# Taking the sum of a left operand one product ahead, in the down products of a two-layer decoder trunk

## The chip, the cores and the metric

The kernel runs on one core of one Trainium2 chip. The metric is the device time of one execution in microseconds (us), the median over the runs. Beside the timed runs there is one profiled execution; all rows of the trace come from it.

## The reference, cut to what matters

The program is a decoder trunk with two layers, 512 positions, a model width of 1024 and a feed-forward width of 2816, all in float32. Each layer is a mixer (a gated convolution with sliding-window attention in layer 0, gated linear attention with latent attention in layer 1), a layer norm, a SwiGLU feed-forward block and a second layer norm. What the change touches is the last matrix product of the feed-forward block:

```
def swiglu(x, w_gate, w_up, w_down):
    return (jax.nn.silu(x @ w_gate) * (x @ w_up)) @ w_down
...
x = layer_norm(ALPHA * x + swiglu(x, ffn_w_gate[layer], ffn_w_up[layer], ffn_w_down[layer]), ...)
```

Every product is made nearly exact by splitting both operands: hi is the operand rounded to TensorE's fp32r type, lo is what the rounding left, and hi x hi + hi x lo + lo x hi is accumulated.

## The kernel before, in words

**The feed-forward block.** The hidden width of 2816 is 22 tiles of 128. Tiles 0 and 1 are computed directly, the other 20 as 10 pairs by a scheme in which seven products of half-size blocks stand for eight (`sevens`, lines 650 to 770; its matmuls are on L713). The results, the hidden tiles, lie in `hs`, each 128 x 512, some in the pool `wk` and some in a large tile that the trace calls `m`.

**The down products.** `seven_down` (L532) multiplies hidden pairs 0 to 7 by their rows of `w_down` by the same kind of scheme. They form four quads q = 0 to 3. For each quad, `hs[DIRECT + q]` gives the blocks a11 and a21 and `hs[DIRECT + QUADS + q]` gives a12 and a22. There are seven products for each quad, named by a position pos, 28 in all, in the order of `seq` (L542). I number them i = 0 to 27:

```
        seq = [(2, 0), (2, 1), (1, 0), (1, 1), (2, 2), (5, 0), (1, 2), (5, 1), (1, 3), (2, 3), (5, 2), (6, 0),
               (5, 3), (6, 1), (6, 2), (6, 3), (3, 0), (3, 1), (3, 2), (3, 3), (7, 0), (7, 1), (7, 2), (7, 3),
               (4, 0), (4, 1), (4, 2), (4, 3)]
```

The left operand of positions 1, 2 and 4 is a block as it is (a11, a12, a22). That of positions 5, 6, 3 and 7 is a sum of blocks, and in 16 of the 28 products VectorE therefore has a sum to take first. For positions 5, 6 and 3 it is kept in place in one of four slices of a tile `ssum` (position 5 sets a22 - a21, position 6 adds a11, position 3 subtracts a12); for position 7 it is a fresh tile from the pool `tmp`. Between i = 10 and i = 23 every product has a sum. `ssum` takes over the buffer of `xl0`, the lo part of the block's input, when `sevens` has done with it.

**make(i), L571.** It prepares both operands of product i. On SyncE's queue, `load(i + 4)` starts the transfer of a piece of weights into one of five `raw` buffers. Then the instructions are, in this order:

- ScalarE: hi of the weights, 128 x 1024 (L100, `w<-raw`)
- VectorE: lo of the weights, 128 x 1024 (L106, `w<-raw,w`)
- VectorE: the sum, 128 x 512, where there is one (L585, L587, L589 or L592)
- ScalarE: hh, the hi part of the left operand, 128 x 512 (L100, or L594 for position 6, `hx<-...`)
- VectorE: hl, its lo part, 128 x 512 (L106, or L595)

**take(i), L600.** It is TensorE's part: 12 matmuls on L613 with 512 columns each, six into one PSUM bank (b = 0) and then six into another (b = 1). After the last quad of a position come copies out of these banks: for position 1 two to `tmp` (L628), for position 5 two to `p5` (L619), for positions 6 and 7 two from the bank into a fresh bank (L623), all on ScalarE; for positions 3 and 7 two on VectorE (L632), and for position 2 two more (L635). The copy of position 6 reads the two banks `d` into which position 3, the very next product, goes on to accumulate.

**The order.** In `ffn` (L450) the order of every engine and queue is the order in which the code is written. The loop at its end calls make(i) and then take(i - AHEAD), AHEAD = 4, so that on ScalarE the copies of take(i) stand behind all of make(i + 4). The operand pair hi and lo lies in a pool `wp` of five buffers, so make(i) can't start before take(i - 5) has ended; hh and hl lie in the pool `hx` of twelve. What comes behind (`down`, L336, with its matmuls on L349, and the mixer of the next layer) is ordered by hand on TensorE only; on the other engines a planner of the language arranges it by estimated costs and due times.

Of the kernel before, what the change touches and what calls it, by code (L numbers as in the profile page):

```python
# [11 lines left out]
F32R = mybir.dt.float32r  # L12
# [34 lines left out]
def trunk(ctx, tc, a, out):  # L47
# [22 lines left out]
    def nm(s):  # L70
        cnt[0] += 1
        return f"{s}{cnt[0]}"
# [4 lines left out]
    def slot2(dt=F32):  # L77
        return hx.tile([P, 512], dt, tag="hx", name=nm("hx"))

    def temp(tag="tmp", dt=F32):  # L80
        return tmp.tile([P, 512], dt, tag=tag, name=nm(tag))
# [4 lines left out]
    def ps():  # L86
        return psp.tile([P, 512], F32, tag="ps", name=nm("ps"))
# [11 lines left out]
    def split(src, hi, lo, pool=False):  # L99
        nc.scalar.copy(out=hi, in_=src)  # L100
        if pool:
            n = src.shape[1] // 2
            for c in (slice(0, n), slice(n, 2 * n)):
                nc.gpsimd.tensor_tensor(out=lo[:, c], in0=src[:, c], in1=hi[:, c].bitcast(F32), op=ALU.subtract)
            return
        tt(out=lo, in0=src, in1=hi.bitcast(F32), op=ALU.subtract)  # L106

    def pair(n=D):
        t = wp.tile([P, 2, D], F32R, tag="w", name=nm("w"))
        return t[:, 0, :n], t[:, 1, :n]  # L110
# [17 lines left out]
    def renew():  # L128
        for t, n in ((xh, "xh"), (xl, "xl")):
            t[:] = t or [None, None]  # L130
            for j in range(2):
                if t[j] is None:
                    t[j] = big.tile([P, 4, S], F32R, tag=f"{n}{j}", name=nm(n))
# [398 lines left out]
    def seven_down(hs):  # L532

        base = state["i"]
        state["i"] += 4 * QUADS
        raw, ops = {}, {}
        s_ = {}

        g = {}
# [4 lines that stand above are left out]
        def piece(which, q):  # L546
            i = base + 4 * q + ("11", "12", "21", "22").index(which)
            return a["w"][i // 2, :, (i % 2) * D:(i % 2) * D + D]


        t_ = {(n, q): dram.tile([P, D], F32, tag=f"t{n}{q}", name=nm("t")) for n in (1, 2, 3, 4) for q in range(QUADS)}

        def copy(n, q, src):
            nc.gpsimd.dma_start(out=t_[n, q], in_=piece(src, q) if isinstance(src, str) else t_[src, q])

        def add(n, q, which):
            nc.gpsimd.dma_start(out=t_[n, q], in_=piece(which, q), accum_op=ALU.add)

        steps = [lambda f=f, n=n, q=q, w=w: f(n, q, w)
                 for f, n, w in ((copy, 1, "11"), (add, 1, "12"), (copy, 3, "22"), (add, 3, "12"), (copy, 2, 1),  # L560
                                 (add, 2, "22"), (copy, 4, 2), (add, 4, "21")) for q in range(QUADS)]

        def load(i):
            if not 0 <= i < len(seq):
                return
            pos, q = seq[i]
            raw[i] = rawp.tile([P, D], F32, tag="raw", name=nm("raw"))
            src = {1: "11", 2: "21", 3: "22", 5: 1, 6: 2, 7: 3, 4: 4}[pos]
            nc.sync.dma_start(out=raw[i], in_=piece(src, q) if isinstance(src, str) else t_[src, q])

        def make(i):  # L571

            load(i + 4)
            if not s_:
                s = big.tile([P, 4, S], F32, tag="xl0", name=nm("ssum"))
                s_.update({q: s[:, q, :] for q in range(QUADS)})
                xl[0] = None
            pos, q = seq[i]
            (a11, a21), (a12, a22) = hs[DIRECT + q], hs[DIRECT + QUADS + q]
            hi, lo = pair()  # L580
            split(raw.pop(i), hi, lo)
            hh, hl = slot2(F32R), slot2(F32R)
            x = {1: a11, 2: a12, 4: a22, 7: None}.get(pos, s_.get(q))
            if pos == 5:
                tt(out=x, in0=a22, in1=a21, op=ALU.subtract)  # L585
            elif pos == 6:
                tt(out=x, in0=x, in1=a11, op=ALU.add)  # L587
            elif pos == 3:
                tt(out=x, in0=x, in1=a12, op=ALU.subtract)  # L589
            elif pos == 7:  # L590
                x = temp()
                tt(out=x, in0=a11, in1=a21, op=ALU.subtract)  # L592
            if pos == 6:
                act(out=hh, in_=x, func=AF.Copy, scale=-1.0)  # L594
                stt(out=hl, in0=x, scalar=-1.0, in1=hh.bitcast(F32), op0=ALU.mult, op1=ALU.subtract)  # L595
            else:
                split(x, hh, hl)
            ops[i] = hi, lo, hh, hl

        def take(i):  # L600

            pos, q = seq[i]
            hi, lo, hh, hl = ops.pop(i)
            name = {2: "a", 1: "d", 5: "b", 6: "d", 3: "d", 7: "e", 4: "f"}[pos]
            if name not in g:
                g[name] = [ps(), ps()]
            fresh = q == 0 and pos in (1, 2, 5)
            for b in range(2):
                bank = g[name][b]
                for k in range(2):  # L610
                    t, c = slice(k * 256 + b * P, k * 256 + b * P + P), slice(k * 512, k * 512 + 512)
                    for m, (l, r) in enumerate(((hh, hi), (hh, lo), (hl, hi))):
                        mm(bank, lhsT=l[:, t], rhs=r[:, c], start=(fresh and k == 0 and m == 0),  # L613
                           stop=(k == 1 and m == 2), skip_group_check=True)
                if q < QUADS - 1:
                    continue
                if pos == 5:
                    g.setdefault("p5", []).append(temp("p"))
                    nc.scalar.copy(out=g["p5"][b], in_=bank)  # L619
                elif pos in (6, 7):  # L620
                    to = "e" if pos == 6 else "f"
                    g.setdefault(to, []).append(ps())
                    nc.scalar.copy(out=g[to][b], in_=bank)  # L623
            if q == QUADS - 1:
                for b in range(2):
                    if pos == 1:
                        g["p1"] = temp()
                        nc.scalar.copy(out=g["p1"], in_=g["d"][b])  # L628
                        g.setdefault("sum", []).append((b, g["p1"]))
                    elif pos in (3, 7):  # L630
                        bank = g[name][b]
                        stt(out=bank, in0=bank, scalar=-1.0, in1=g["p5"][b], op0=ALU.mult, op1=ALU.subtract)  # L632
            if pos == 2 and q == QUADS - 1:
                for b, t in g["sum"]:
                    tt(out=g["a"][b], in0=g["a"][b], in1=t, op=ALU.add)  # L635

        acc = {}

        def last(f):
            f()  # L640
            renew()
            acc.update({b: [g["a"][b], g["d"][b]] for b in range(2)})
            acc.update({b + 2: [g["f"][b], g["e"][b]] for b in range(2)})

        n = len(seq)
        takes = [lambda i=i: take(i) for i in range(n)]
        takes[-1] = lambda: last(lambda: take(n - 1))
        return acc, [lambda i=i: make(i) for i in range(n)], takes, load, steps

    def sevens(sx, hs, hidden_tile):  # L650
# [787 lines left out]
```

## Time and profile before

| | |
|---|---|
| median of three runs | 1081.66 us (1081.38 to 1081.66) |
| profiled execution, device time | 1080.37 us |
| its span, first to last instruction | 1078.6 us |
| mean granted TensorE clock | 0.987 |
| TensorE matmul / weight load busy | 97% / 88% of the span |
| VectorE / ScalarE / GpSimd busy | 73% / 50% / 10% |
| matmuls of the down products (L613) | 672, in two stretches: 400.6 to 490.2 us and 948.5 to 1037.3 us |
| GpSimd in these two stretches | no instruction |

In the rows, PE is TensorE's matmul, PEld its weight load, DVE is VectorE, ACT ScalarE, POOL GpSimd, SPq SyncE's queue of transfers. A group of instructions reads "out<-in" by the program's names. In a timeline the columns are start, time covered, engine, line, operation, operands, count, and in brackets how long the engine sat idle before it and what released it. Instructions of an engine overlap a little, so the step from one start to the next is less than the duration. One product starts on TensorE every 2.73 us while nothing holds it.

### The profile page before, as it was taken

Reading aid. Unit: us, or ns where it says so; the run is one execution under the profiler, and the core shown is the slowest. Engines: PE = TensorE matmul, PEld = TensorE weight load, DVE = VectorE, ACT = ScalarE, POOL = GpSimd, SP = SyncE. Lnnn points to the kernel's source line nnn. Section 1 sums busy time; section 2 is a strip of 40 time slices with the busy share of each in tenths; the row PEclk is TensorE's granted clock in tenths of the full one; section 3 lists DMA queues with packets and bytes.
Section 4 is the critical chain, followed back from the end, with each engine's and each line's share of the span. In section 5 each row is a group of like instructions: output and inputs, shape, how many; then the busy total and the mean of one; then the engine's idle time right before and its main releaser. Section 6 shows DMA issues by size and latency. Waiting matters only on the chain.

```text
span 1078.6 us, 17142 instructions
## 1 busy us (share of the span) xinstructions
PE 1046.4 (97%) x6861; PEld 946.5 (88%) x6861; DVE 792.5 (73%) x1180; ACT 543.4 (50%) x896; POOL 103.5 (10%) x162
## 2 busy tenths in 40 slices
PE   9999999999999999599999999999999999997796
PEld 7888889999999998488988888889999999986685
DVE  5666549888787777684857886479887787786757
ACT  5544335655545465463467454355655554554541
POOL 0000001222000000000513420003120000000000
PEclk9999999999999999799999999999999999999899
DMA  9522222999624355453232031228997323364422
GB/s 335 203 77 79 78 79 61 286 300 286 180 80 136 99 165 187 138 172 101 98 137 78 2 118 36 76 68 221 310 310 216 115 79 124 113 234 136 140 76 78
DMA packets 42960, 156.60 MB, mean 145 GB/s; under 512 B 4976, under 2 KB 5632, under 8 KB 42624
## 3 DMA queue, kind: packets, MB, share of 16 engines
q1 hardware_dynamic: 35168, 120.89, 33.1%
q0 software_dynamic: 7712, 34.61, 12.7%
q8 instruction: 54, 0.88, 0.3%
q14 instruction: 26, 0.21, 0.1%
HBM read 153.38 MB, written 35.65 MB: 175 GB/s over the span
## 4 chain that ended last, share of the span: by engine, by line
PE 90%; DVE 5%; ACT 3%; issue 1%; DMA 0%; SPq 0%; POOL 0%; DVEq 0%; ACTq 0%; POOLq 0%
PE ps L713 37%; PE ps L193 16%; PE ps L349 13%; PE ps L613 9%; PE ps L227 6%; DVE w L106 2%; ACT w L100 2%; PE ps L1162 1%; PE ps L289 1%; PE ps L1087 1%; PE ps L1010 1%; PE ps L859 1%; PE ps L806 1%; PE ps L846 1%; PE ps L1060 0%
## 5 line engine op out<-in xcount | busy, mean ns | idle before, releaser
L106 DVE TENSOR_TENSOR w<-raw,w 128x1024 fp32r<-128x1024 f32 (+2 forms) x206 | 249.2, 1214 | 77.3 <-ACT w L100 72.2
L100 ACT CAST w<-raw 128x1024 fp32r<-128x1024 f32 (+3 forms) x209 | 215.0, 1035 | 79.2 <-PE ps L713 17.0
L713 PE MATMUL ps<-xh,w 128*128 128x256 f32 x1280 | 237.5, 283 | 0.0
L713 PEld LDWEIGHTS ps<-xh,w 128*128 128x128 f32 x1280 | 202.7, 192 | 0.0
L713 PE MATMUL ps<-xl,w 128*128 128x256 f32 x640 | 181.1, 283 | 0.0
L713 PE MATMUL ps<-hx,w 128*128 128x256 f32 x1440 | 179.6, 283 | 0.0
L613 PE MATMUL ps<-w,hx 128*128 128x512 f32 x672 | 156.8, 396 | 21.9 <-ACT ps L623 21.9
L713 PEld LDWEIGHTS ps<-hx,w 128*128 128x128 f32 x1440 | 175.9, 192 | 0.1
L613 PEld LDWEIGHTS ps<-w,hx 128*128 128x128 f32 x672 | 128.4, 192 | 49.7 <-ACT ps L623 22.8
L193 PE MATMUL ps<-xh,w 128*128 128x512 f32 (+1 forms) x608 | 161.0, 348 | 0.2 <-ACT xh L100 0.2
L349 PE MATMUL ps<-w,hx 128*128 128x512 f32 x657 | 151.9, 391 | 0.0
L349 PEld LDWEIGHTS ps<-w,hx 128*128 128x128 f32 x657 | 122.7, 188 | 25.1
L713 PEld LDWEIGHTS ps<-xl,w 128*128 128x128 f32 x640 | 122.8, 192 | 0.3
L193 PEld LDWEIGHTS ps<-xh,w 128*128 128x128 f32 x608 | 106.4, 189 | 15.3 <-ACT xh L100 0.7
L193 PE MATMUL ps<-xl,w 128*128 128x512 f32 (+1 forms) x304 | 105.0, 345 | 0.2 <-DVE xl L106 0.2
L266 POOL TENSOR_TENSOR rs<-ve,neghalf 128x1 f32<-128x1 f32 x15 | 9.2, 611 | 713.5 <-DVE ve L264 675.2
L193 PEld LDWEIGHTS ps<-xl,w 128*128 128x128 f32 x304 | 57.6, 190 | 7.2 <-DVE xl L106 0.8
L227 PE MATMUL ps<-w,xh 128*128 128x512 f32 (+1 forms) x192 | 58.6, 386 | 0.0
L106 DVE TENSOR_TENSOR w<-lnb,w 128x1024 fp32r<-128x1024 f32 x30 | 36.7, 1225 | 17.8 <-ACT w L100 17.7
L106 DVE TENSOR_TENSOR w<-lng,w 128x1024 fp32r<-128x1024 f32 x30 | 36.7, 1224 | 16.4 <-ACT w L100 16.4
L106 DVE TENSOR_TENSOR hx<-m,hx 128x512 fp32r<-128x512 f32 x32 | 21.3, 688 | 31.8 <-ACT hx L100 31.8
L227 PEld LDWEIGHTS ps<-w,xh 128*128 128x128 f32 x192 | 35.2, 188 | 5.0
(249 smaller groups left out, 1244.2 us busy)
## 6 DMA issues: line engine op xcount, KB each, us to landing
raw<-in_w_dram SPq DMA_DIRECT2D x174, 512.0 KB, 4.8
t<-in_w_dram POOLq DMA_DIRECT2D x48, 512.0 KB, 11.1
raw<-t SPq DMA_DIRECT2D x32, 512.0 KB, 3.3
t<-t POOLq DMA_DIRECT2D x16, 512.0 KB, 13.0
hx<-in_xT_dram SPq DMA_DIRECT2D x8, 256.0 KB, 6.2
xn<-in_xn_dram SPq DMA_DIRECT2D x4, 512.0 KB, 9.4
out_dram<-xn SPq DMA_DIRECT2D x7, 256.0 KB, 2.0
lng<-in_ln_mix_g_dram SPq DMA_DIRECT2D x2, 512.0 KB, 7.5
```

Of the source, the lines that this page charges most:

```text
L100: nc.scalar.copy(out=hi, in_=src)
L106: tt(out=lo, in0=src, in1=hi.bitcast(F32), op=ALU.subtract)
L193: mm(dst[:, cols], lhsT=l[:, k, :], rhs=xk(r, k, cols), start=(k == 0 and n == 0), stop=(k == KD - 1 and n == 2))
L227: mm(banks[b][:, :n], lhsT=xk(l, k, t), rhs=r[:, c], start=(k == 0 and m == 0), stop=(k == KD - 1 and m == 2))
L289: nc.tensor.transpose(tp[:, k * P:(k + 1) * P], xn[:, b, h * 512 + k * P:h * 512 + (k + 1) * P], ident)
L349: mm(acc[b][h], lhsT=l(b), rhs=r[:, h * 512:h * 512 + 512], start=(not begun and k == 0 and n == 0), stop=(k == ends[b, h] and n == 2), sk ...
L613: mm(bank, lhsT=l[:, t], rhs=r[:, c], start=(fresh and k == 0 and m == 0), stop=(k == 1 and m == 2), skip_group_check=True)
L713: mm(bank[:, f * 256:f * 256 + 256], lhsT=l[:, f, k, :], rhs=r[k // 2][:, k % 2, :], start=(start and f == 0 and k == 0 and m == 0), stop= ...
L806: mm(banks[s][bank][:, o:o + n], lhsT=l[rows[s], b * P:(b + 1) * P], rhs=r[rows[s], (b + 1) * P - n:(b + 1) * P], start=(i == 0), stop=(i ...
L846: nc.tensor.transpose(bank[:, o:o + P], src, ident)
L859: mm(po[rows[s], b * P:(b + 1) * P], lhsT=vn[:, j * P + 64 * s:j * P + 64 * s + 64], rhs=loc[s][(b, half)], start=(half == 0 or b == 0), s ...
L1010: mm(dst, lhsT=x[:, c], rhs=y, start=(k == 0 and n == 0), stop=(k == nk - 1 and n == 2))
```

## The change

`make` is cut in two. The sum of product i is taken by a new function `total(i)`, and make(i) calls total(i + 1) between its own lo of the weights and its own hh. The result waits in a dictionary `left` until make(i + 1) uses it. make(0) calls total(0) itself, and the buffer `ssum` is now taken in the first `total`. VectorE's order in make(i) is then lo of the weights i, sum of product i + 1, hl of product i. In the order of the program, hh of product i stands behind the sum of product i + 1. No instruction is added or removed, and nothing else changes its place.

```diff
-        def make(i):
-
-            load(i + 4)
+        left = {}
+
+        def total(i):
+
+            if i >= len(seq):
+                return
             if not s_:
                 s = big.tile([P, 4, S], F32, tag="xl0", name=nm("ssum"))
                 s_.update({q: s[:, q, :] for q in range(QUADS)})
                 xl[0] = None
             pos, q = seq[i]
             (a11, a21), (a12, a22) = hs[DIRECT + q], hs[DIRECT + QUADS + q]
-            hi, lo = pair()
-            split(raw.pop(i), hi, lo)
-            hh, hl = slot2(F32R), slot2(F32R)
-            x = {1: a11, 2: a12, 4: a22, 7: None}.get(pos, s_.get(q))
+            x = {1: a11, 2: a12, 4: a22}.get(pos, s_[q])
             if pos == 5:
                 tt(out=x, in0=a22, in1=a21, op=ALU.subtract)
             elif pos == 6:
...
             elif pos == 7:
                 x = temp()
                 tt(out=x, in0=a11, in1=a21, op=ALU.subtract)
+            left[i] = x
+
+        def make(i):
+
+            load(i + 4)
+            pos, q = seq[i]
+            hi, lo = pair()
+            split(raw.pop(i), hi, lo)
+            if i == 0:
+                total(0)
+            x = left.pop(i)
+            total(i + 1)
+            hh, hl = slot2(F32R), slot2(F32R)
             if pos == 6:
                 act(out=hh, in_=x, func=AF.Copy, scale=-1.0)
                 stt(out=hl, in0=x, scalar=-1.0, in1=hh.bitcast(F32), op0=ALU.mult, op1=ALU.subtract)
```

## The prediction

> **What bounds the kernel now.** I read the page first, then the waits of the whole run, then the timeline of the two stretches in which the down products run, then the engine windows around them. The page says that TensorE sets the time:
>
> ```profile
> span 1078.6 us, 17142 instructions
> ...
> PE 1046.4 (97%) x6861; PEld 946.5 (88%) x6861; DVE 792.5 (73%) x1180; ACT 543.4 (50%) x896; POOL 103.5 (10%) x162
> ...
> PE 90%; DVE 5%; ACT 3%; issue 1%; DMA 0%; SPq 0%; POOL 0%; DVEq 0%; ACTq 0%; POOLq 0%
> ...
> L613 PE MATMUL ps<-w,hx 128*128 128x512 f32 x672 | 156.8, 396 | 21.9 <-ACT ps L623 21.9
> ```
>
> TensorE is busy for 97% of the span, yet the chain that ended last runs over DVE and ACT for 8% of it, and the down products' matmuls stand idle for 21.9 us behind a copy on ScalarE, L623. The waits tell how often, and what ScalarE itself waited for:
>
> ```profile
> PE ps L613 <- ACT ps L623: 21.9, 2, 11.0
> ...
> ACT hx L594 <- DVE ssum L587: 16.9, 8, 2.8
> ...
> ACT hx L100 <- DVE tmp L592: 15.2, 8, 1.9
> ACT hx L100 <- DVE ssum L585: 15.2, 8, 1.9
> ACT hx L100 <- DVE ssum L589: 15.2, 8, 1.9
> ```
>
> So there are two stalls of 11 us, one in each layer, and ScalarE waited 32 times for a sum on VectorE before an hh, once for each product with a sum. The timeline of layer 1 shows how the one makes the other:
>
> ```profile
> 948.51 43.71 PE L613 MATMUL ps<-w,hx 128*128 128x512 f32 x192
> ...
> 951.45 1.06 ACT L100 CAST w<-raw 128x1024 fp32r<-128x1024 f32 x1 [0.63 <-PE ps L613]
> ...
> 965.10 1.05 ACT L100 CAST w<-raw 128x1024 fp32r<-128x1024 f32 x1 [1.14 <-issue]
> ...
> 995.63 1.04 ACT L100 CAST w<-raw 128x1024 fp32r<-128x1024 f32 x1
> ...
> 999.09 1.04 ACT L100 CAST w<-raw 128x1024 fp32r<-128x1024 f32 x1
> ...
> 1000.16 1.23 DVE L106 TENSOR_TENSOR w<-raw,w 128x1024 fp32r<-128x1024 f32 x1 [0.25 <-ACT w L100]
> 1001.30 0.69 DVE L589 TENSOR_TENSOR ssum<-ssum,m 128x512 f32<-128x512 f32 x1
> 1002.02 0.62 ACT L100 CAST hx<-ssum 128x512 fp32r<-128x512 f32 x1 [1.90 <-DVE ssum L589]
> 1002.54 1.06 ACT L623 COPY ps<-ps 128x512 f32<-128x512 f32 x2
> 1002.67 0.69 DVE L106 TENSOR_TENSOR hx<-ssum,hx 128x512 fp32r<-128x512 f32 x1 [0.68 <-ACT hx L100]
> 1003.18 34.27 PE L613 MATMUL ps<-w,hx 128*128 128x512 f32 x144 [10.96 <-ACT ps L623]
> ```
>
> TensorE does 16 products in 43.71 us, 2.73 each. The hi casts at 951.45 (i = 5) and 965.10 (i = 10) start 0.2 us after take(0) and take(5) end (948.51 + 2.73 and + 6 x 2.73): so far make is as early as its five buffers allow. From i = 10 on every product has a sum, and then a ring holds: hi, lo of the weights, sum, hh, next hi. The last two casts of the row, i = 18 and 19, are 3.46 us apart. ScalarE thus loses 0.73 us per product against TensorE, and more at its copies. When TensorE ends take(15), at 948.51 + 43.71 = 992.2, ScalarE isn't even at make(18). The copies of take(15) stand behind make(19), take(16) writes into the bank they read, and TensorE waits until the first is done at 1003.18. The stall isn't a lack of prepared operands; it is the lateness of ScalarE's queue. It costs the clock as well:
>
> ```profile
> 455.23 35.11 PE L613 MATMUL ps<-w,hx 128*128 128x512 f32 x144 [10.97 <-ACT ps L623]
> ```
>
> ```profile
> 300.00:400.00 100.00, 100.00 (x836) 100.00 (x835) 76.67 (x76) 53.34 (x69) 0.00 (x0) 1.00 0.35 114
> 444.30:455.20 10.90, 0.00 (x0) 0.00 (x0) 7.34 (x9) 5.22 (x9) 0.00 (x0) 0.59 0.39 129
> 455.20:466.10 10.90, 10.87 (x38) 8.82 (x39) 6.33 (x8) 4.67 (x6) 0.00 (x0) 0.79 0.35 131
> ```
>
> The granted clock (the column before the last two) is 1.00 in a busy stretch, 0.59 in the stall and 0.79 in the 10.9 us behind it. The 144 matmuls after the stall should take 144/192 x 43.71 = 32.78 us; they took 35.11 and 34.27, which is 2.33 and 1.49 more.
>
> **The change part by part.** Nothing is added or removed: 32 sums of 0.69 us move on VectorE, each to the place after the lo of the weights of the product before. No transfer moves: load(i + 4) stays first in make(i), and neither SyncE's nor GpSimd's queue is passed.
>
> *ScalarE.* hh(i) now uses a sum taken one product earlier, so it can follow hi(i) at once. The steps of a make and of the copies without such a wait stand in the trace, at position 4:
>
> ```profile
> 1023.93 1.06 ACT L100 CAST w<-raw 128x1024 fp32r<-128x1024 f32 x1 [1.15 <-issue]
> 1024.89 0.61 ACT L100 CAST hx<-m 128x512 fp32r<-128x512 f32 x1
> 1025.41 0.58 ACT L623 COPY ps<-ps 128x512 f32<-128x512 f32 x1
> ...
> 1026.61 0.57 ACT L623 COPY ps<-ps 128x512 f32<-128x512 f32 x1
> ```
>
> hi to hh is 0.96 us and hh to the next 0.52, together 1.48 per product against TensorE's 2.73. These are also the copies of position 7, the same pattern as those that stall, and TensorE runs through them (its 144 matmuls stand in one row): with make at its limit such copies cost nothing.
>
> *VectorE.* Its steps where nothing is waited for:
>
> ```profile
> 1018.13 0.69 DVE L106 TENSOR_TENSOR hx<-tmp,hx 128x512 fp32r<-128x512 f32 x1 [0.69 <-ACT hx L100]
> 1018.74 1.29 DVE L632 SCALAR_TENSOR_TENSOR ps<-ps,p 128x512 f32<-128x512 f32 x2
> 1019.93 1.22 DVE L106 TENSOR_TENSOR w<-raw,w 128x1024 fp32r<-128x1024 f32 x1
> 1021.07 0.69 DVE L106 TENSOR_TENSOR hx<-wk,hx 128x512 fp32r<-128x512 f32 x1
> 1021.67 1.22 DVE L106 TENSOR_TENSOR w<-raw,w 128x1024 fp32r<-128x1024 f32 x1
> ```
>
> lo of the weights to the next 1.14, a 512-column instruction to the next 0.61, hl to lo 0.60: 1.14 + 0.61 + 0.60 = 2.35 per product with a sum, 0.38 below TensorE's 2.73. The 0.68 before hl goes too, since hh(i) ends (0.96 + 0.62 = 1.58 after hi) before hl(i) can start (1.08 + 1.14 + 0.61 = 2.83; 1.08 is 999.09 to 1000.16). One burden comes between, the two additions of L635 behind make(13):
>
> ```profile
> 980.69 1.29 DVE L635 TENSOR_TENSOR ps<-ps,tmp 128x512 f32<-128x512 f32 x2
> ```
>
> 1.29 us, paid back at 0.38 a product in four products, before make(19).
>
> *New waits.* The sum now stands ahead of hl(i), which is 0.61 later. Behind it queue lo(i + 1) and so on; who waits for hl(i) is take(i). At the limit hl(10) ends 2.83 + 0.69 = 3.5 after hi, at 968.6, and take(10) starts at 948.51 + 10 x 2.73 = 975.8: 7 us of cover. Without it each of the 32 sums would cost up to 0.61. The first sum needs the buffer of `ssum`, whose last matmuls, those of `sevens`, lie before 948.5, while the sum falls at make(4), after 951. A raw piece must land within the time from its issue:
>
> ```profile
> raw<-in_w_dram SPq DMA_DIRECT2D x174, 512.0 KB, 4.8
> ...
> raw<-t SPq DMA_DIRECT2D x32, 512.0 KB, 3.3
> ```
>
> load(i + 4) is issued when lo(i - 1) frees its buffer, 2.3 us after hi(i - 1), and used five products later, 13.7 after it: over 11 us for 4.8. These three cost nothing.
>
> *At the stall.* take(14) ends at 948.51 + 15 x 2.73 = 989.5. hi(19) starts at 989.7 (999.09 now), hh(19) at 990.6 (its sum, in make(18), is done at about 989.8), the first copy at 991.2, done 991.7. take(16) wants that bank at 992.2. The second copy starts when take(15) ends, is done at 993.0, and is wanted half a product after 992.2, at 993.6. Spare: 0.5 and 0.6 us. Both stalls go, and the slow clock with them. What is late next is nothing on this path: from 1023.93 on, make is at its buffer limit in the trace of before too (that cast starts when take(22) ends), so the work behind is met in the same relative state. There a planner arranges DVE and ACT and may choose anew; I put this at nothing, with one product's 2.73 us either way as bound.
>
> *Sum.* 10.97 + 10.96 of idle time and 2.33 + 1.49 of slow matmuls, 25.75 us. The profiled execution took 1080.37 us, 1.8 beyond its span; its span becomes 1052.9 and its time 1054.6. The median is 1.3 above that execution, so 1081.66 - 25.75 = 1055.9 us.
>
> **The rivals.** *VectorE becomes the bound.* The Trainium skill, "VectorE: DVE Perf Modes", section "The DRAIN you can't avoid", says that the next VectorE instruction does not start until the pipeline has emptied; the rows above do not bear it out to the full duration, as L632 starts 0.61 after an hl of 0.69. As a mechanism here: full durations, 1.23 + 0.69 + 0.69, and the 0.25 before lo make 2.86, 0.13 over TensorE. Over nine products that is 1.2, with L635 2.5 us of lateness. hh(19) can be 0.8 late and the first copy 0.5 more; 1.2 of stall would remain in each layer, 1058.3. If instead the 0.68 before hl stayed (1.14 + 0.61 + 0.68 + 0.60 = 3.03), lateness is 9 x 0.30 + 1.29 = 4.0, the stall 2.7 per layer, and with a quarter of the clock's toll 1062. Against it: everything in the steps quoted.
>
> *The change doesn't do what it says.* `ssum` is one tile of four slices, and in program order hh(i) now stands behind the sum of i + 1, which writes another slice. If waits went by the whole tile, hh(i) would wait for that sum, at the same place as now: the ring of 3.46 stays, ten products long as before, and the time is 1081.7. Against it stands layer 0's first products, where matmuls read token columns of `xh` while a cast ahead of them in program order writes others:
>
> ```profile
> 177.27 1.04 PE L289 MATMUL ps<-pack,xn 128*128 128x128 f32 x8
> ...
> 177.90 1.08 ACT L294 CAST xh<-ps 128x512 fp32r<-128x512 f32 x2 [2.75 <-PE ps L289]
> ...
> 178.06 0.36 PE L193 MATMUL ps<-xh,w 128*128 128x256 f32 x1
> ```
>
> L193 starts at 178.06, while the casts run until 178.98: waits go by region.
>
> *Slower: the clock.* The stalls are TensorE's rest. If the granted clock fell to the 0.79 of the row above in the longer unbroken run, each us would lose 0.21. At 80 us in each layer that is 34 us, 1089.5; it decides from 25.75 / 0.21 = 123 us in all. Against it: 1.00 over 100 us without a gap.
>
> **How the numbers follow.** Full effect 0.85, at 1055.9; VectorE bound 0.08, 1058 to 1062; no effect 0.05, 1081.7; slower 0.02. The range takes the planner's 2.73 below, 1053.2, and the VectorE rival's end above, 1062. About 0.2%, 2 us, is what a measurement of this kernel can tell from no change; faster by more 0.93, within it 0.05, slower 0.02.
>
> **What would show it.** Right: no idle time before L613, its 336 matmuls of a layer in one row of about 76.5 us, no ACT wait for L585, L587, L589 and L592, hh 0.96 after hi, a clock of 1.00 throughout these stretches. Wrong: a wait of hh for a sum at the old 1.9 (whole-tile rival), an idle time before L613 of 1 to 3 us with ACT waiting little (VectorE), or matmuls longer at a lower clock.

## The result, and the profile after

The median fell from 1081.66 us to 1054.70 us (four runs each; 1054.18 to 1055.51 after), a ratio of 0.9752 with a 95% interval of 0.9735 to 0.9769. The forecast was 1055.9, in a range of 1053.2 to 1062.0. The profiled execution took 1055.16 us, its span 1053.4. L613 of before is L626 now, L623 is L636, L635 is L648 and L594 is L607.

The lines of the page that answer to those of before:

```profile
span 1053.4 us, 17142 instructions
...
PE 1042.9 (99%) x6861; PEld 944.1 (90%) x6861; DVE 789.0 (75%) x1180; ACT 543.9 (52%) x896; POOL 103.3 (10%) x162
...
PE 97%; DVE 1%; DMA 1%; ACT 0%; SPq 0%; issue 0%; POOL 0%; DVEq 0%; ACTq 0%; POOLq 0%
...
L626 PE MATMUL ps<-w,hx 128*128 128x512 f32 x672 | 152.7, 389 | 0.0
```

The number of instructions is the same. The idle time before the down products' matmuls went from 21.9 us to none, their busy time from 156.8 to 152.7 us, and VectorE and ScalarE, which held 8% of the chain of waits, hold 1%. The timeline of layer 1 around the copies of product 15 shows how:

```profile
935.88 76.35 PE L626 MATMUL ps<-w,hx 128*128 128x512 f32 x336
...
964.50 1.29 DVE L648 TENSOR_TENSOR ps<-ps,tmp 128x512 f32<-128x512 f32 x2
965.70 1.22 DVE L106 TENSOR_TENSOR w<-raw,w 128x1024 fp32r<-128x1024 f32 x1
...
967.55 0.63 ACT L607 ACTIVATE hx<-ssum 128x512 fp32r<-128x512 f32 x1 [0.42 <-DVE ssum L587]
968.04 1.22 DVE L106 TENSOR_TENSOR w<-raw,w 128x1024 fp32r<-128x1024 f32 x1
...
970.38 1.22 DVE L106 TENSOR_TENSOR w<-raw,w 128x1024 fp32r<-128x1024 f32 x1
...
972.91 0.61 ACT L100 CAST hx<-ssum 128x512 fp32r<-128x512 f32 x1
...
974.19 0.68 DVE L589 TENSOR_TENSOR ssum<-ssum,m 128x512 f32<-128x512 f32 x1
...
976.95 1.05 ACT L100 CAST w<-raw 128x1024 fp32r<-128x1024 f32 x1 [1.15 <-issue]
...
977.91 0.61 ACT L100 CAST hx<-ssum 128x512 fp32r<-128x512 f32 x1
...
978.43 0.58 ACT L636 COPY ps<-ps 128x512 f32<-128x512 f32 x1
...
979.63 0.57 ACT L636 COPY ps<-ps 128x512 f32<-128x512 f32 x1 [0.62 <-PE ps L626]
```

All 336 matmuls of the layer stand in one row. ScalarE now idles 1.15 us before hi(19), at 976.95. The row names no releaser, but take(14), which frees the buffer that hi(19) needs, ends at 935.88 + 15 x 2.73 = 976.8: hi(19) is as early as it may be. The two copies are done at 979.0 and 980.2. At 76.35/28 = 2.73 us a product, TensorE wants the first bank at 935.88 + 16 x 2.73 = 979.5 and the second at 980.9. The second copy even waits for take(15) to end. Layer 0 has the same row, and the granted clock (before the last two columns) is full in both stretches:

```profile
401.02 76.35 PE L626 MATMUL ps<-w,hx 128*128 128x512 f32 x336
```

```profile
401.00:477.00 76.00, 76.00 (x338) 62.94 (x337) 65.77 (x82) 49.17 (x66) 0.00 (x0) 1.00 0.65 205
...
935.90:1012.00 76.10, 76.10 (x338) 63.02 (x337) 65.87 (x82) 49.18 (x66) 0.00 (x0) 1.00 0.61 193
```

From the first down product to the first matmul of what follows, layer 0 took 490.17 - 400.55 = 89.6 us and takes 477.21 - 401.02 = 76.2; layer 1 took 88.8 and takes 76.2. That is 13.4 + 12.6 = 26.0 us. The span fell by 25.2, since the rest of the kernel was 0.8 us slower in this execution, 0.5 of it before the first down product is reached.

### The profile page after: what moved, and what is told of

It reads as the page before. It is cut to its first block, busy times and chain, and to the rows that moved or that the text cites. A ratio compares the mean times of both kernels' runs of the same rounds, so it can differ in the third digit from the quotient of the medians.

```text
span 1053.4 us, 17142 instructions
## 1 busy us (share of the span) xinstructions
PE 1042.9 (99%) x6861; PEld 944.1 (90%) x6861; DVE 789.0 (75%) x1180; ACT 543.9 (52%) x896; POOL 103.3 (10%) x162
## 3 DMA queue, kind: packets, MB, share of 16 engines
q0 software_dynamic: 7712, 34.61, 13.1%
## 4 chain that ended last, share of the span: by engine, by line
PE 97%; DVE 1%; DMA 1%; ACT 0%; SPq 0%; issue 0%; POOL 0%; DVEq 0%; ACTq 0%; POOLq 0%
PE ps L726 38%; PE ps L193 16%; PE ps L626 14%; PE ps L349 13%; PE ps L227 6%; PE ps L1175 1%; PE ps L289 1%; PE ps L1100 1%; PE ps L1023 1%; PE ps L872 1%; DMA hx<-in_xT_dram 1%; PE ps L819 1%; PE ps L859 1%; PE ps L1073 0%; PE ps L1089 0%; PE ps L1071 0%
## 5 line engine op out<-in xcount | busy, mean ns | idle before, releaser
L626 PE MATMUL ps<-w,hx 128*128 128x512 f32 x672 | 152.7, 389 | 0.0
L349 PE MATMUL ps<-w,hx 128*128 128x512 f32 x657 | 151.9, 391 | 0.0
L626 PEld LDWEIGHTS ps<-w,hx 128*128 128x128 f32 x672 | 126.0, 188 | 26.1
L193 PEld LDWEIGHTS ps<-xh,w 128*128 128x128 f32 x608 | 106.3, 189 | 15.6 <-DVE w L106 0.4
```

Of the source, the lines that this page charges most:

```text
L193: mm(dst[:, cols], lhsT=l[:, k, :], rhs=xk(r, k, cols), start=(k == 0 and n == 0), stop=(k == KD - 1 and n == 2))
L349: mm(acc[b][h], lhsT=l(b), rhs=r[:, h * 512:h * 512 + 512], start=(not begun and k == 0 and n == 0), stop=(k == ends[b, h] and n == 2), sk ...
```

## The experiments

The theory that I tested I call the ring theory: ScalarE is made late by the ring hi, lo, sum, hh, hi in products 10 to 19, and TensorE feels it only where the copies of product 15 stand behind make(19). The first rival is that the gain comes by share, a part for each sum that an hh no longer waits for. Each run was compared with runs of the kernel before on the same chip, whose median was 1081.5 to 1081.8 us.

### Only the sums of position 7

```diff
-            if i == 0:
-                total(0)
+            if pos not in (7,):
+                total(i)
+            if i + 1 < len(seq) and seq[i + 1][0] in (7,):
+                total(i + 1)
             x = left.pop(i)
-            total(i + 1)
```

> Only the sums of position 7 (i = 20 to 23) are taken one product ahead; those of positions 5, 6 and 3 stand in their old place. Ring theory (what costs is how late ScalarE reaches the copies of product 15, which stand behind make(19)): these sums come after that point, so the idle time before the down products' matmuls stays at 11.0 us in each layer and the time at 1081.7, within 1.5. Rival, by share (each sum that an hh no longer waits for gives its part of the whole, 27.0/32 = 0.84 us): 8 sums, 6.7 us, 1074.9.

Measured: 1082.11 us, ratio 1.000 (0.9991 to 1.0009). The matmuls of the down products, as a group (busy time and mean ns, then idle time before them and its releaser), and the two stalls:

```profile
L627 PE MATMUL ps<-w,hx 128*128 128x512 f32 x672 | 157.6, 397 | 21.9 <-ACT ps L637 21.9
```

```profile
455.49 35.73 PE L627 MATMUL ps<-w,hx 128*128 128x512 f32 x144 [10.95 <-ACT ps L637]
...
1004.35 34.47 PE L627 MATMUL ps<-w,hx 128*128 128x512 f32 x144 [10.96 <-ACT ps L637]
```

The stalls are there in full. Eight hh no longer wait 1.9 us, and it is worth nothing: those products come after the copies that matter. The sharing rival falls.

### Only positions 5 and 6, only position 3

The same edit with (5, 6) and with (3,) in place of (7,).

> Only the sums of positions 5 and 6 (i = 5, 7, 10 to 15) are taken ahead; positions 3 and 7 keep the old order. Ring theory: make is at its buffer limit up to 16, then four rings with the copies of position 5 among them bring the first copy of product 15 to 14.8 us after hi(16), as before, where take(15) ends 10.7 after it; with 0.6 for the copy an idle time of about 4.7 us in each layer, 9.4 in all, and some of the slow clock behind it, 1 us a layer: 1066, within 1.5. Rival, by share: 16 of 32 sums, 13.5 us, 1068.2 with an idle time of 5.5 a layer. The two lie close here; the idle time and where it lies decide less than in the other runs.

> Only the sums of position 3 (i = 16 to 19) are taken ahead; 5, 6 and 7 keep the old order. Ring theory: the rings from 10 to 15 leave hi(16) 6.4 us behind its limit; from there ScalarE needs 2.5 and then VectorE 2.35 a product, so the copies come about 4.5 us after take(15) ends: idle 4.5 in each layer, 9 in all, and about 2 us of slow clock, 1065.7, within 2. Rival, by share: 8 sums, 6.7 us, 1074.9 with an idle time of about 8 a layer.

Measured: 1069.25 us (ratio 0.9886, 0.9872 to 0.9901) and 1068.61 us (0.9881, 0.9866 to 0.9895). First (5, 6), then (3,), each with its group and then the stalls in the timeline:

```profile
L627 PE MATMUL ps<-w,hx 128*128 128x512 f32 x672 | 159.0, 399 | 9.3 <-ACT ps L637 9.3
```

```profile
448.49 35.76 PE L627 MATMUL ps<-w,hx 128*128 128x512 f32 x144 [4.67 <-ACT ps L637]
...
991.09 35.80 PE L627 MATMUL ps<-w,hx 128*128 128x512 f32 x144 [4.67 <-ACT ps L637]
```

```profile
L627 PE MATMUL ps<-w,hx 128*128 128x512 f32 x672 | 157.1, 396 | 8.8 <-ACT ps L637 8.8
```

```profile
449.16 34.32 PE L627 MATMUL ps<-w,hx 128*128 128x512 f32 x144 [4.39 <-ACT ps L637]
...
989.72 35.31 PE L627 MATMUL ps<-w,hx 128*128 128x512 f32 x144 [4.37 <-ACT ps L637]
```

The idle times are those that the ring gives, 4.67 where 4.7 was expected and 4.4 where 4.5 was. For (3,) the sharing rival had about 8. Half of the sums and a quarter of them each take off more than half of the idle time, 12.6 and 13.1 us of 21.9, together more than the whole; no share can do that. But both times came out 3 us too long and outside what I had allowed (1.5 and 2 us), and for (5, 6) the time alone lies nearer to the rival's 1068.2; it is the idle time that speaks for the ring. The rows say where the 3 us are: the 144 matmuls behind the stall, 32.7 us at full clock (144/336 x 76.35), took 34.3 to 35.8. The slow clock cost 1.6 to 3.1 us a layer where I had put 1. A stall of 4.5 us costs the clock as much as one of 11.

### The copies earlier in ScalarE's queue, the sums as before

```diff
                 i -= AHEAD
                 if i < n:
                     take(i)
-                else:
+                elif i - n == 13:
+                    for j in (13, 14, 15):
+                        takes[j]()
+                elif i - n not in (14, 15):
                     takes[i - n]()
```

> The kernel before with its sums in the old place; only the takes of products 14 and 15 are written ahead of make(18), so that the two copies of product 15 stand behind make(17) in ScalarE's queue and not behind make(19). Ring theory: the copies start at 995.6 in layer 1 in place of 1002.5, the idle time at that point falls from 11.0 to about 4.0 us; but the ring goes on at 3.46 against 2.73, make(18) and (19) come 1 us later than before, and TensorE runs out of operands from about product 20: another 2 to 3 us of idle time spread before products 20 to 23, with hl or hh as releaser. In all 6.6 a layer in place of 11: 1071, within 3. Rival, the place in the queue is the whole cause: idle 4.0 a layer and nothing later, 1065 or less. Rival, the place doesn't matter, since preparation itself is what TensorE lacks: 1081.7.

Measured: 1081.06 us, ratio 0.9993 (0.9984 to 1.0003). The ring theory's 1071 missed by 10 us. The time is that of the last rival, 1081.7, but the rows show that its mechanism isn't what happened. The group, and TensorE's rows of layer 1:

```profile
L616 PE MATMUL ps<-w,hx 128*128 128x512 f32 x672 | 162.3, 404 | 15.9 <-ACT ps L626 15.8 <-ACT hx L100 0.2
```

```profile
949.57 43.71 PE L616 MATMUL ps<-w,hx 128*128 128x512 f32 x192
997.32 21.12 PE L616 MATMUL ps<-w,hx 128*128 128x512 f32 x84 [4.04 <-ACT ps L626]
1018.61 3.26 PE L616 MATMUL ps<-w,hx 128*128 128x512 f32 x12 [0.17 <-ACT hx L100]
1025.91 12.75 PE L616 MATMUL ps<-w,hx 128*128 128x512 f32 x48 [4.04 <-ACT ps L626]
```

The first stall fell to 4.04, as the ring theory had it: the place of the copies in the queue does decide when it ends, and TensorE hardly ever lacks an operand. The ring goes on behind it, and what TensorE gained is lost again eight products later, not through the lack of operands that I had expected (0.17 us) but at the next copies, those of product 23 behind make(27). Idle time is 6.0 us less than before in all. Yet the busy time of the matmuls is 5.5 us more, because the clock falls twice in each layer. In layer 1:

```profile
997.30:1005.00 7.70, 7.68 (x26) 6.16 (x27) 4.82 (x7) 3.92 (x6) 0.00 (x0) 0.78 0.39 130
...
1027.00:1039.50 12.50, 12.50 (x52) 10.25 (x51) 10.09 (x13) 6.15 (x9) 0.00 (x0) 0.91 0.37 121
```

Two stalls of 3.7 to 4.0 us cost as much as one of 11. Without the ring's cure the place in the queue is worth nothing.

### The sum one product ahead, but behind hl

```diff
             x = left.pop(i)
-            total(i + 1)
...
+            total(i + 1)
             ops[i] = hi, lo, hh, hl
```

> The sum of product i + 1 is still taken one product ahead, but behind hl of product i, not between lo of the weights and hl. Ring theory: what matters is that the sum is done before hh(i + 1) can start, not where on VectorE it stands; it ends about 3.5 us after hi(i), hh(i + 1) starts 3.7 after it at TensorE's pace. No idle time before the down products' matmuls, 1054.7 within 1 us (no difference of 0.2%). Rival, the place between the two lo's is needed because it fills VectorE's wait for hh: hl then waits for hh again, up to 0.7 a product, idle time comes back, 2 us a layer, 1058.5 or more.

Measured: 1054.76 us, 0.1 us from the kernel after (ratio to before 0.9755, 0.9740 to 0.9769). One row of 336 matmuls again, and ScalarE's longest wait for a sum in layer 1:

```profile
935.60 76.35 PE L626 MATMUL ps<-w,hx 128*128 128x512 f32 x336
```

```profile
967.87 0.63 ACT L606 ACTIVATE hx<-ssum 128x512 fp32r<-128x512 f32 x1 [1.03 <-DVE ssum L587]
```

The place between the two lo's isn't what brings the gain; taking the sum in the make before is. The later place leaves less in hand (a wait of 1.03 in place of 0.42 behind the two additions), and none of it reaches TensorE.

### More work on VectorE

The kernel after, with hl written a second time where the product has a sum, by 256 columns as here or by all 512:

```diff
+            if pos == 6:
+                stt(out=hl[:, :256], in0=x[:, :256], scalar=-1.0, in1=hh[:, :256].bitcast(F32), op0=ALU.mult, op1=ALU.subtract)
+            elif pos in (5, 3, 7):
+                tt(out=hl[:, :256], in0=x[:, :256], in1=hh[:, :256].bitcast(F32), op=ALU.subtract)
             ops[i] = hi, lo, hh, hl
```

> The kernel after, with 256 columns of hl written a second time in every product with a sum: 0.34 us more on VectorE each, 10.9 us in all. Ring theory: VectorE then needs 2.35 + 0.34 = 2.69 a product, just under TensorE's 2.73, but it can't pay back the 1.29 us of the two additions of L648 before product 19; hh(19) may be late by 0.8 and the copy by 0.5 more, so 0 to 0.3 us of idle time a layer: 1054.7 to 1055.5. Rival, VectorE's work lies on the path: 10.9 us more, 1065.6.

> The kernel after, with all 512 columns of hl written a second time in every product with a sum: 0.61 us more on VectorE each, 19.5 us in all. Ring theory: 2.35 + 0.61 = 2.96 a product is 0.23 over TensorE's 2.73; ten products and the 1.29 of L648 make 3.6 us of lateness, less 1.25 of slack 2.3 us of idle time a layer before product 16, some more with the copies of product 23, and up to 1 us of slow clock: 1059 to 1062. Rival, VectorE's work lies on the path: 19.5 us more, 1074.2.

Measured: 1057.21 us (ratio to before 0.9777, 0.9763 to 0.9792) and 1062.09 us (0.9827, 0.9811 to 0.9844), so 2.5 and 7.4 us over the kernel after. First the group, TensorE's stall of layer 0 and VectorE's rows of one product with 256 columns, then the group and the stalls with 512:

```profile
L630 PE MATMUL ps<-w,hx 128*128 128x512 f32 x672 | 153.3, 389 | 1.5 <-ACT ps L640 1.5
```

```profile
445.01 32.94 PE L630 MATMUL ps<-w,hx 128*128 128x512 f32 x144 [0.76 <-ACT ps L640]
...
966.70 1.21 DVE L106 TENSOR_TENSOR w<-raw,w 128x1024 fp32r<-128x1024 f32 x1
...
968.43 0.68 DVE L608 SCALAR_TENSOR_TENSOR hx<-ssum,hx 128x512 fp32r<-128x512 f32 x1
969.15 0.42 DVE L612 SCALAR_TENSOR_TENSOR hx<-ssum,hx 128x256 fp32r<-128x256 f32 x1
969.49 1.22 DVE L106 TENSOR_TENSOR w<-raw,w 128x1024 fp32r<-128x1024 f32 x1
```

```profile
L630 PE MATMUL ps<-w,hx 128*128 128x512 f32 x672 | 154.9, 392 | 5.4 <-ACT ps L640 5.4
```

```profile
446.95 32.96 PE L630 MATMUL ps<-w,hx 128*128 128x512 f32 x144 [2.70 <-ACT ps L640]
...
984.47 34.55 PE L630 MATMUL ps<-w,hx 128*128 128x512 f32 x144 [2.70 <-ACT ps L640]
```

The 10.9 us of added work that I had reckoned cost 2.5, the 19.5 cost 7.4: VectorE's work isn't on the path; what counts is how much it has in hand at each product. Both came out above what was expected, and the rows show why. The second write starts 0.72 us after the first (968.43 to 969.15), not 0.61, as it waits for it to finish. A product takes 969.49 - 966.70 = 2.79 us on VectorE, just over TensorE's 2.73 and not just under: none of the 1.29 us of the two additions is paid back, and lateness grows a little at each product. The copies come too late by 0.8 us in each layer. With 512 columns a product takes 3.07 us, likewise 0.11 more than reckoned, and the stall is 2.70 in place of 2.3.

### Only the ten sums of products 10 to 19

```diff
-            if i == 0:
-                total(0)
+            if not 10 <= i < 20:
+                total(i)
+            if 10 <= i + 1 < 20:
+                total(i + 1)
             x = left.pop(i)
-            total(i + 1)
```

> Only the ten sums of products 10 to 19 are taken one product ahead; those of products 5, 7 and 20 to 23 keep the old place (in each layer 6 of 16). Ring theory: the ring makes ScalarE late only from product 10 on, and only what is late by product 19 reaches TensorE; the ring of 20 to 23 starts from the buffer limit, loses 0.73 a product, 2.9 us, and products 24 to 27, which ScalarE prepares in 1.48 each against 2.73, pay that back before the copies of product 23. No idle time before the down products' matmuls, 1054.7 within 1.5. Rival, by share: 20 of 32 sums, 16.9 us of the 27.0, 1064.8 with 4 us of idle time a layer.

Measured: 1054.37 us, ratio 0.9747 (0.9730 to 0.9763): all of the gain with ten of the sixteen sums of a layer.

```profile
L627 PE MATMUL ps<-w,hx 128*128 128x512 f32 x672 | 152.7, 389 | 0.0
```

```profile
982.27 0.62 ACT L100 CAST hx<-tmp 128x512 fp32r<-128x512 f32 x1 [1.89 <-DVE tmp L592]
...
998.89 0.61 ACT L100 CAST hx<-m 128x512 fp32r<-128x512 f32 x1
999.41 0.58 ACT L637 COPY ps<-ps 128x512 f32<-128x512 f32 x1
```

In products 20 to 23 ScalarE still waits 1.89 us for each sum, and TensorE doesn't notice: products 24 to 27 pay the lateness back before the copies of product 23 at 999.41.

### The runs in one table

The idle and the busy time of the 672 matmuls come from the group rows; "slow" is the busy time over the 152.7 us of the kernel after. Idle and slow together account for each median to within about 1 us:

| kernel | idle | slow | sum | median over 1054.7 |
|---|---|---|---|---|
| before | 21.9 | 4.1 | 26.0 | 27.0 |
| only position 7 | 21.9 | 4.9 | 26.8 | 27.4 |
| copies earlier | 15.9 | 9.6 | 25.5 | 26.4 |
| only 5 and 6 | 9.3 | 6.3 | 15.6 | 14.6 |
| only 3 | 8.8 | 4.4 | 13.2 | 13.9 |
| 512 columns more | 5.4 | 2.2 | 7.6 | 7.4 |
| 256 columns more | 1.5 | 0.6 | 2.1 | 2.5 |
| sum behind hl | 0.0 | 0.0 | 0.0 | 0.1 |
| ten sums | 0.0 | 0.0 | 0.0 | -0.3 |

## Why the prediction was right

**The stall and its cause.** It was read from the trace as the lateness of ScalarE's queue, made by the ring, at copies that stand behind make(19). The ten-sums run, the run with position 7 alone and the one with earlier copies show each part of this: the ring of products 10 to 19 makes the lateness, what comes later doesn't matter while it is paid back, and the copies' place in the queue is where it reaches TensorE.

**What hides the moved sums.** VectorE's 2.35 a product against 2.73 was the term on which the forecast stood. In the kernel after it is 2.34 where nothing is waited for (965.70 to 968.04 to 970.38), and the burden of the two additions appears as foreseen and is paid back. It shows as one wait of 0.42 us in each layer (at 967.55 in layer 1), which the list of signs ("no ACT wait for" a sum) had left out. The run with 256 columns more shows how narrow the reserve is: 0.45 us a product uses it up.

**The times at the stall.** Counted from the start of product 0, the first copy was forecast to end 43.2 us on and the second 44.5; they ended 43.1 and 44.3 us on (978.43 + 0.58 and 979.63 + 0.57, less 935.88). Spare was 0.5 and 0.7 where 0.5 and 0.6 were forecast.

**The sum.** 25.75 us were forecast, 26.0 us left the two stretches. The profiled execution was forecast at 1054.6 us and took 1055.16. The forecast of the median is 1.2 us too high because I carried over the 1.3 us by which the median lay above the profiled execution, and after the change the median lies 0.5 below it.

**The rivals.** Waits by the whole tile: hh starts at 972.91, the sum ahead of it in program order, on another slice of `ssum`, at 974.19, so no. The clock falling in the longer run: 1.00 throughout, no. VectorE as the bound: not here, but 0.45 us a product away, and then near the price of its mechanism: 1.5 us of idle time at 2.79 us a product and 5.4 at 3.07, where the prediction had reckoned 2.4 at 2.86 and 5.4 at 3.03. The planner's part, which I had bounded at one product, kept its order on every engine; only on SyncE's queue the load of `wgate` moved by one place.

## What to carry to other kernels

When an engine with 97% busy time still stalls, look for the queue on which its release stands, and for what delays that whole queue, not the releasing instruction: here a copy of 0.57 us was 11 us late because of a ring through ScalarE and VectorE in the ten products before it. Here the ring was opened by taking one of its links a product earlier, and only its turns before the releasing instruction counted. A stall that is only shortened may still pay for the clock in full: with 12.6 or 13.1 us of idle time gone, the slow clock cost 6.3 or 4.4 us where it had cost 4.1. A stall split in two paid twice, and of 6 us of idle time saved nothing was left.

## What the runs showed of the hardware

From some 4 us on, the price of the clock doesn't grow with the stall. Behind stalls of 0.8 us nothing to speak of was lost (0.2 us of 32.7). Behind stalls of 2.70 us in one execution, layer 0 lost 0.2 us and layer 1 lost 1.8; behind 4.4 to 4.7 us the loss was 1.6 to 3.1, behind 11 us, before and with position 7 alone, 1.6 to 3.0.

The granted clock shows why. In these traces it is 1.00 or 0.50 and nothing between; means like the 0.59 and 0.79 of the prediction mix the two. In layer 0 of the kernel before, the stall lasted from 444.26 to 455.23:

```profile
444.30:446.20 1.90, 0.00 (x0) 0.00 (x0) 0.90 (x1) 0.97 (x2) 0.00 (x0) 1.00 0.26 99
446.20:455.20 9.00, 0.00 (x0) 0.00 (x0) 6.44 (x9) 4.25 (x7) 0.00 (x0) 0.50 0.41 135
455.20:459.90 4.70, 4.67 (x11) 3.71 (x12) 2.74 (x4) 2.05 (x3) 0.00 (x0) 0.50 0.39 140
459.90:466.10 6.20, 6.20 (x28) 5.12 (x28) 3.60 (x4) 2.62 (x3) 0.00 (x0) 1.00 0.33 124
```

The clock fell 2.0 us after the stall began and stayed at half for 13.65 us in one piece, of which 4.65 lay behind the stall. Half of 4.65 is 2.3, and 2.4 us were lost. The pieces at half clock that go with the stalls of all these runs last 3.41, 6.83, 10.24 or 13.65 us, one to four times 3.41. What a stall costs is thus half of what such a piece leaves behind it, not a share of its own length. In the kernel with 512 columns more, layer 1, the granted clock in the stall and behind it was:

```profile
981.00:984.40 3.40, 0.76 (x4) 0.30 (x2) 3.37 (x5) 1.91 (x4) 0.00 (x0) 1.00 0.46 164
984.40:988.00 3.60, 3.53 (x9) 2.85 (x10) 3.57 (x6) 2.09 (x4) 0.00 (x0) 0.53 0.63 229
988.00:992.00 4.00, 4.00 (x19) 3.29 (x18) 3.96 (x6) 1.68 (x3) 0.00 (x0) 1.00 0.47 151
```

In layer 0 of the same run it stayed full behind a stall of the same length:

```profile
447.00:455.00 8.00, 8.00 (x35) 6.63 (x36) 7.93 (x12) 4.72 (x7) 0.00 (x0) 1.00 0.51 179
```

In layer 1 the clock is halved for 3.41 us from the end of the stall on, and not in it. Counted back from there in steps of 3.413 us, the gap of layer 1 (981.77 to 984.47) lies within one step, while that of layer 0 (444.25 to 446.95) is cut by a border at 445.2 into 0.9 and 1.8 us; this fits the two outcomes, but no run tests it. The Trainium skill, "TensorE: Matmul & The Clock Gate", Part 1, describes a window of about 3.4 us that runs freely, half the clock after at least one idle window and the full clock after a busy one. The length of the slow pieces agrees, and so does it that equal gaps can cost differently. That the gap must fill a window is not borne out: one of 2.70 us halved the clock in one layer, and in the kernel before the clock fell 2.0 us into the stall; there the measurement decides.
